# A hybrid attention and pooling layer on one core: the means of the pooling mixer by two operations a product from values kept in DRAM, each gate's job behind its group's values, and pooling sums later

## The chip, the cores and the metric

The kernel runs on one core of a Trainium2 chip. A core has a matrix engine (TensorE, here PE; its weight loads are PEld), a vector engine (VectorE, DVE), an engine for activations, copies and casts (ScalarE, ACT), a general engine (GpSimd, POOL) and one that in this kernel only starts transfers (SyncE, SP). Each engine works through its own instructions in a fixed order and waits, where it must, for the others by semaphores. Transfers (DMAs) are started by an instruction in the queue of SP, POOL or ACT. The metric is the time of the whole program in microseconds on the device; lower is better.

## The reference

One layer, 1024 tokens, width 2048, everything in float32:

```python
h = x @ w_in + b_in
q, k, v, g_attn, u_pool, g_pool = split(h)
a = banded_sink_attention(q, k, v, sinks, bias, valid) * silu(g_attn)
b = multiscale_pool(u_pool, w_pool, pool_scale) * silu(g_pool)
mix = concatenate([a, b]) @ w_out
ple = sigmoid(x @ w_gate_ple) * (p @ w_ple)
out = layer_norm(2 ** 0.25 * x + mix + ple, ln_gain, ln_bias)
```

The pooling mixer has 1024 channels in four groups of 256. Group g takes the mean over the last 2, 4, 8 or 16 tokens (fewer at the start), subtracts the token itself, multiplies by a 256 x 256 matrix of the group and by a scale for each channel.

## The kernel before

**Products.** Activations lie with channels on the 128 partitions and tokens along the free dimension. A float32 matrix is split into a rounded part and a rest (names ending in h and l), and a product of two such matrices is three matmuls (`mm3`, L182 to L184: high by high, high by low, low by high). The large matrix products go by a Strassen scheme with seven products in place of eight. A *job* (class `Job`) takes two blocks of 128 output channels and half of the 2048 input channels, for 1024 tokens in most stages; it is seven products (`product`), and each product is four input blocks by three matmuls of 128x512, so twelve matmuls. Two or three jobs may run interleaved in one group (`run_group`); otherwise a job is its own group. A product's result is taken from PSUM by `gather`: four of a job's seven by a copy on ACT (L402), three by an add on DVE (L125, `part<-part,qa` or `qb`). The weights arrive as `raw`; `make_unit` forms Strassen's sums of them on DVE, casts the high part on ACT (`wh`, L736) and subtracts on DVE (`wl`, L125), four units ahead of their use.

**Stages.** Stage 1 and 2 make the first parts of q, k, v over the two halves of the input channels, stage 2 also the second-half part of all other blocks, which is stored in DRAM (`h`, `g`) and added to the first-half part in stage 3 by an accumulating DMA of POOL (`finished`, L415). Attention itself runs beside stage 2, between about 180 and 700 us. Stage 3 (about 690 to 1125 us) is 20 jobs in the order of the list `rest`: pooling gate and pooling values of group 0 interleaved, then gate 3, values 3, gate 2, values 2, values 1, gate 1; then eight jobs of the embedding gate (`wgate`), then four of the attention gates, the last two interleaved. Stage 4 multiplies by w_out for the second input half, stages 5 and 6 for the first half in two cuts of the tokens (768 and 256), with the sums of squares and the output of the norm beside them.

**The clock of the plan.** The order is written by the program itself: each product is a tick (`tick`), `after(n, f)` emits f's instructions n products later, and `later(n, f)` does that with each of them held behind the last matmul, ACT copy and DVE add of the products so far. When a job ends, its `done` is called by `later(job.wait, ...)`, wait being 4 products for most jobs and 3 for the last pair of stage 3, so that the accumulating DMA can land. `load` starts a DMA from SP's queue, `aside` from POOL's. Engine order and buffers are then settled at build time; a tile drawn from a pool waits until a buffer of that pool is free.

**The steps that the change touches.**
- `set_from` makes the operand sets of stage 1 on DVE (`sub`) and ACT; step s2 splits t1 and forms t2.
- `ple_half` (L778) is early work of the embedding in stage 1; its result leaves PSUM by an ACT copy `b22h<-tr`, `b22h<-pv` (L736 is the helper `copy`).
- `set_kept` loads and splits the operand sets of stage 3's first group.
- `pool_u` (called as `done` of the value jobs): for each of two blocks and both halves of the tokens, ACT adds the bias (L128), DVE doubles the window by one, two, three or four adds (`s<-s`, L125), subtracts the token (L698), and the result is split (ACT `e<-s`, DVE `e<-s,e`). All of it is emitted in one tick. `mix(g)` follows ten or eleven products later: 24 matmuls into the two `sc` banks, each result multiplied with the gate that `gate_pool` stored (`sgp`).
- `pool_sums` fetches four pieces of the mixer's result (`s<-cc`) two ticks into the embedding's jobs 4, 6, 8, 10, forms four differences (`s<-s,s`) on DVE two ticks after that and stores them (`pt<-s`) for stage 4.
- `embed`, `embed_ahead`, `embed_w`: the embedding's gate, its fetched values, its weights.
- `gate_attn`: silu on ACT (L666), two multiplications on DVE by the fetched attention output (`gate_ahead`, `s<-pre`), and a store `cc<-part` from POOL's queue.
- `norm_square` (L921), `norm_scale`, `norm_out`: the norm's steps in stages 5 and 6.

Results of jobs lie in five buffers `part`; small tiles of stage 3 in 16 buffers `s` and six `e`, ten `s` at its end.

Of the kernel before, what the change touches and what calls it, by code (L numbers as in the profile page):

```python
# [25 lines left out]
F32R = mybir.dt.float32r  # L26
# [25 lines left out]
RAWS = 5  # L52
EARLY = (0, 1, 6, 7)


# [9 lines left out]
class Layer:  # L65
# [203 lines left out]
    def set_from(self, get, F, keep=None, first=None, by=None):  # L269
# [47 lines left out]
        def s2():  # L317
            split("t1")
            sub("t2", "b22", "t1", None if keep else "t1")

# [34 lines left out]

    def pool_sums(self, i, m, keep):

        at = [(4 + i, 0), (4 + i, 1), (6 + i, 0), (6 + i, 1)]
        r = []

        def make():
            b11, b12, b21, b22 = r
            self.tt(b11, b12, b11, ALU.subtract)
            self.tt(b12, b22, b12, ALU.subtract)
            self.tt(b22, b22, b11, ALU.subtract)
            self.tt(b21, b21, b22, ALU.subtract)
            for u, t in (("t1", b11), ("t3", b12), ("t2", b22), ("t4", b21)):
# [295 lines left out]

    def gate_attn(self, j, c):
        nc = self.nc
        nc.scalar.activation(c, c, AF.Silu, bias=self.c(C_BIN + GA0 + j))  # L666
# [9 lines left out]

    def pool_u(self, j, c):
        nc, g = self.nc, j // 2
        w = 2 << g
        out = []  # L680
        for h in range(2):
            u = self.slot()
            if h == 0:
                nc.gpsimd.memset(u[:, 0:16], 0.0)
            else:
                self.ident_act(u[:, 0:16], c[:, 0, T - 16 :], self.c(C_BIN + U0 + j))
            self.ident_act(u[:, 16:], c[:, h], self.c(C_BIN + U0 + j))
            cur, d, first = u, 1, 1
            while d < w:
                nxt = self.slot()  # L690
                end = 2 * d == w
                f = 16 if end else first
                self.tt(nxt[:, f:], cur[:, f:], cur[:, f - d : T + 16 - d], ALU.add)
                cur, d = nxt, 2 * d
                first = first + d
            if h == 0:
                self.tt(cur[:, 16 : 16 + 16], cur[:, 16 : 16 + 16], self.c(C_HEAD + 16 * g, 16), ALU.mult, nc.gpsimd)
            nc.vector.scalar_tensor_tensor(out=cur[:, 16:], in0=cur[:, 16:], scalar=1.0 / w, in1=u[:, 16:],  # L698
                                           op0=ALU.mult, op1=ALU.subtract)
            out.append(self.split(cur[:, 16:], 2 * (j % 2) + h < 3))  # L700
        self.diff[j] = out
        if j % 2:
            f = slice((g % 2) * T, (g % 2) * T + T)
            self.after(4, lambda: self.got.update({("wp", g): self.fetch(self.wpool[g // 2][:, f])}))
            self.later(8, lambda: self.got.update({("wp", g): self.split(self.got["wp", g])}))
            late = 3 if g == 1 else 0
            self.after(6 + late, lambda: self.got.update({("sg", g): [[self.fetch(self.sgp[2 * g + e][:, h * T : h * T + T]) for e in range(2)] for h in range(2)]}))
            self.later(10 + late // 2, lambda: self.mix(g))

# [68 lines left out]
    def ple_half(self, n, h, tags):  # L778
# [13 lines left out]
        for b in range(2):  # L792
            if h:
                self.aside(self.ple[2 * i + b], self.ple_out[(2 * n + b) % 4].rearrange("p h t -> p (h t)"))

    def embed_in(self, r=None):
# [191 lines left out]
    def run(self):  # L988
# [12 lines left out]
        self.sgp = [self.scratch("sgp") for _ in range(8)]  # L1001
        self.r = [self.scratch("r") for _ in range(NB)]
        self.ple = [self.scratch("ple") for _ in range(NB)]
        self.ple_raw, self.turn = {}, {}
# [31 lines left out]
        def consume(w):  # L1036
            def done(b, c):
                if w is wgate:
                    self.embed(b, c)
                elif b >= GP0:  # L1040
                    self.gate_pool(b - GP0, c)
                elif b >= U0:
                    self.pool_u(b - U0, c)
                else:
                    self.gate_attn(b - GA0, c)
            return done
# [20 lines left out]
        s6[-1].mean = True  # L1067
        for j in s4[-2:]:
            j.wait = 6
# [136 lines left out]
        for i in range(n3):  # L1206
# [7 lines left out]
            if i == n3 - 2:  # L1214
# [137 lines left out]
        self.second_done = lambda b, c: self.norm_square(two, b, c)  # L1352
        self.later(3, lambda: self.norm_scale(one, 2))
        for j in range(NB):
            self.later(6 + 18 * j // 16, lambda j=j: self.norm_out(one, j))
        for i in range(8):
# [60 lines left out]
```

## Time and profile before

| | |
|---|---|
| time, median of 3 runs | 1468.27 us |
| the three runs | 1466.94, 1468.27, 1468.92 us |
| profiled execution, own time | 1470.93 us |
| its span, first to last instruction | 1469.2 us |
| mean granted TensorE clock | 0.996 |
| DVE, ACT, POOL busy | 76%, 54%, 20% of the span |
| HBM read, written | 205.62 MB, 94.37 MB |

The page of the profile gives busy times of each engine. PE counts as busy while any matmul is in its pipeline, and two neighbouring matmuls overlap, so short losses don't show as idle time. They show in the number of matmuls that fall into a stretch. The waits of the trace say which instruction stood and whose end released it; a row reads "engine, tile and line <- releaser: us in total, times, longest".

### The profile page before, as it was taken

The page shows a single profiled execution, that of the slowest core. Times are in us where ns is not written, and L with a number is a line of the kernel's source. Part 1 is how long each engine was busy: PE and PEld are TensorE (multiplying, and loading weights), DVE is VectorE, ACT ScalarE, POOL GpSimd, SP SyncE. Part 2 cuts the span into 40 slices and gives each one's busy share as a digit, 9 for nine tenths or more (in the row PEclk, how much of TensorE's full clock was granted, in tenths as well). Part 3 has the DMA queues.
Part 4 walks back from the last instruction along what each step waited for, and adds up shares of the span by engine and source line. Part 5 has one row for each costly group of instructions (what it writes and reads, how often), then busy time and mean ns, then how long its engine had stood idle before and what let it go on. Part 6 is the DMA issues. An engine that isn't in the chain of part 4 may idle for free. (4 is left out here: it accounts for less than half of the span.)

```text
span 1469.2 us, 20535 instructions
## 1 busy us (share of the span) xinstructions
PE 1437.4 (98%) x6930; PEld 1214.9 (83%) x6930; DVE 1120.8 (76%) x2031; ACT 787.3 (54%) x1564; POOL 294.4 (20%) x416
## 2 busy tenths in 40 slices
PE   9999999999999999999999999999999999999996
PEld 7788888888888888887887788788877788899996
DVE  6869578878788797888668785867678566987786
ACT  6546376565575665566545444333456333554475
POOL 1000203332233333223010111211011111111223
PEclk9999999999999999999999999999999999999998
DMA  9463875554456554557765669899698678595475
GB/s 354 173 241 117 244 216 177 178 167 151 138 179 213 188 172 165 186 180 265 191 190 149 166 179 320 260 288 275 189 335 278 184 179 232 134 263 124 120 243 200
DMA packets 109993, 301.35 MB, mean 205 GB/s; under 512 B 12544, under 2 KB 18048, under 8 KB 109888
## 3 DMA queue, kind: packets, MB, share of 16 engines
q1 hardware_dynamic: 84672, 217.46, 43.4%
q0 software_dynamic: 21888, 75.25, 21.2%
q10 hardware_dynamic: 3328, 7.34, 1.5%
q8 instruction: 54, 0.88, 0.2%
q14 instruction: 51, 0.42, 0.1%
HBM read 205.62 MB, written 94.37 MB: 204 GB/s over the span
## 5 line engine op out<-in xcount | busy, mean ns | idle before, releaser
L736 ACT CAST wh<-raw 128x512 fp32r<-128x512 f32 x428 | 263.9, 619 | 400.5 <-PE qa L183 125.6
L125 DVE TENSOR_TENSOR wl<-raw,wh 128x512 fp32r<-128x512 f32 x428 | 300.0, 704 | 102.7 <-ACT wh L736 97.6
L402 ACT COPY part<-qa 128x512 f32<-128x512 f32 (+1 forms) x180 | 103.7, 576 | 74.9 <-PE qa L184 74.4
L620 POOL TENSOR_SCALAR_AFFINE_SELECT s<-s 128x512 fp32r<-128x512 f32 x128 | 102.4, 812 | 132.0 <-ACT s L613 96.5
L125 DVE TENSOR_TENSOR part<-part,qb 128x512 f32<-128x512 f32 (+1 forms) x120 | 81.1, 676 | 44.7 <-PE qb L184 40.1
L182 PE MATMUL qa<-b11h,wh 128*128 128x512 f32 (+2 forms) x292 | 109.4, 375 | 0.4 <-ACT wh L736 0.4
L182 PE MATMUL qb<-b21h,wh 128*128 128x512 f32 (+2 forms) x292 | 109.3, 374 | 0.0
L184 PE MATMUL qa<-b11h,wl 128*128 128x512 f32 (+2 forms) x292 | 108.8, 373 | 0.0
L184 PE MATMUL qb<-b21h,wl 128*128 128x512 f32 (+2 forms) x292 | 108.8, 372 | 0.0
L183 PE MATMUL qa<-b11l,wh 128*128 128x512 f32 (+2 forms) x292 | 108.7, 372 | 0.0
L183 PE MATMUL qb<-b21l,wh 128*128 128x512 f32 (+2 forms) x292 | 108.6, 372 | 0.0
L182 PE MATMUL qb<-t1h,wh 128*128 128x512 f32 (+1 forms) x260 | 100.8, 388 | 3.4 <-DVE part L125 1.6
L182 PE MATMUL qa<-t2h,wh 128*128 128x512 f32 (+1 forms) x260 | 101.1, 389 | 3.0 <-ACT wh L736 1.8
L182 PE MATMUL qa<-t4h,wh 128*128 128x512 f32 (+1 forms) x260 | 100.7, 387 | 2.7 <-DVE part L125 2.7
L182 PE MATMUL qa<-t3h,wh 128*128 128x512 f32 (+1 forms) x260 | 100.6, 387 | 1.6 <-ACT part L402 1.6
L184 PE MATMUL qa<-t2h,wl 128*128 128x512 f32 (+1 forms) x260 | 100.1, 385 | 1.8 <-DVE wl L125 1.8
L182 PE MATMUL qb<-b22h,wh 128*128 128x512 f32 (+1 forms) x260 | 100.5, 386 | 0.5 <-ACT part L402 0.5
L183 PE MATMUL qa<-t3l,wh 128*128 128x512 f32 (+1 forms) x260 | 99.8, 384 | 0.0
L184 PE MATMUL qb<-t1h,wl 128*128 128x512 f32 (+1 forms) x260 | 99.7, 384 | 0.0
L184 PE MATMUL qa<-t4h,wl 128*128 128x512 f32 (+1 forms) x260 | 99.7, 384 | 0.0
L183 PE MATMUL qa<-t2l,wh 128*128 128x512 f32 (+1 forms) x260 | 99.7, 383 | 0.0
L184 PE MATMUL qb<-b22h,wl 128*128 128x512 f32 (+1 forms) x260 | 99.7, 383 | 0.0
(327 smaller groups left out, 3567.2 us busy)
## 6 DMA issues: line engine op xcount, KB each, us to landing
raw<-in_win SPq DMA_DIRECT2D x65, 512.0 KB, 4.3
h<-part SPq DMA_DIRECT2D x34, 512.0 KB, 2.9
part<-h POOLq DMA_DIRECT2D x34, 512.0 KB, 6.6
cw<-in_wout SPq DMA_DIRECT2D x64, 256.0 KB, 3.0
raw<-in_wgate SPq DMA_DIRECT2D x32, 512.0 KB, 4.4
raw<-wc SPq DMA_DIRECT2D x32, 512.0 KB, 4.3
s<-in_x SPq DMA_DIRECT2D x44, 256.0 KB, 5.9
wc<-cw SPq DMA_DIRECT2D x32, 256.0 KB, 2.4
```

What stands on the lines that cost most here:

```text
L125: return (eng or self.nc.vector).tensor_tensor(out=out, in0=a, in1=b, op=op)
L182: mm(ps, wh, xh, start=start, stop=False, skip_group_check=True)
L183: mm(ps, wh, xl, start=False, stop=False, skip_group_check=True)
L184: return mm(ps, wl, xh, start=False, stop=stop, skip_group_check=True)
L402: self.mark("ACT", self.nc.scalar.copy(out=dst, in_=ps))
L620: nc.gpsimd.affine_select(out=o4, in_=a4, pattern=[[0, 4], [sign, P]], compare_op=ALU.is_ge, fill=0.0, base=0 if side else -1, channel_mul ...
L736: ins = self.nc.scalar.copy(out=out, in_=a)
```

## The change

In stage 1, t2 is formed two products later; and the ACT copies after one of the early embedding pieces are held in order behind its output. The operand sets of stage 3's first group are split half a set at a time, in two neighbouring products. The differences of `pool_sums` are formed two each at 7 and 8 ticks in place of four at 4. `pool_u` stores the values with their bias in DRAM (`ud`) from SP, keeps the first block on chip, fetches the second one back, and emits the chain of adds, subtraction and rest two operations a product; the mix follows when they are through, or 13 or 14 products after. In the order of stage 3's jobs the values of groups 3 and 2 come ahead of their gates. The two jobs of attention gates ahead of the last pair wait five products, fetch the attention output earlier, and store from SP one product later. The embedding's weights are split four products after their fetch, not two. The jobs of stage 5 but the last two wait six products for their sum, and the norm's first scale is spread one product later.

```diff
+POOL_MIX = {3: 13, 2: 14, 1: 13}
...
         def s2():
             split("t1")
-            sub("t2", "b22", "t1", None if keep else "t1")
+            if first:
+                self.later(2, lambda: sub("t2", "b22", "t1", None))
+            else:
+                sub("t2", "b22", "t1", None if keep else "t1")
...
         def step(i):
             u = UNITS[BESIDE[i]]
-            self.split_unit(u, r.pop(u))
-            fetch(i + 2)
+            pieces = r.pop(u)
+            self.split_unit(u, [])
+            for n in range(2):
+                self.split_part(u, n, pieces[n])
+
+            def rest():
+                for n in range(2, 4):
+                    self.split_part(u, n, pieces[n])
+                fetch(i + 2)
+
+            if i:
+                self.after(1, rest)
+            else:
+                rest()
...
-        self.later(4, make)
+        for second in range(2):
+            self.later(7 + second, lambda second=second: make(second))
...
-    def gate_attn(self, j, c):
+    def gate_attn(self, j, c, soon):
...
-        self.aside(self.cc[j // 2][:, j % 2], c.rearrange("p h t -> p (h t)"))
+        store = lambda by: by(self.cc[j // 2][:, j % 2], c.rearrange("p h t -> p (h t)"))
+        if soon:
+            self.after(1, lambda: store(self.load))
+        else:
+            store(self.aside)
...
     def pool_u(self, j, c):
+        g = j // 2
+        self.ident_act(c, c, self.c(C_BIN + U0 + j))
+        if j % 2 == 0:
+            self.pool_first = [self.slot() for _ in range(2)]
+            self.nc.gpsimd.memset(self.pool_first[0][:, 0:16], 0.0)
+            self.nc.scalar.copy(out=self.pool_first[1][:, 0:16], in_=c[:, 0, T - 16 :])
+            for h in range(2):
+                self.nc.scalar.copy(out=self.pool_first[h][:, 16:], in_=c[:, h])
+        self.load(self.ud[j], c.rearrange("p h t -> p (h t)"))
+        if j % 2 == 0:
+            return
+        self.diff[j - 1], self.diff[j] = [None, None], [None, None]
+        begin = max(0, self.pool_free - self.clock)
+        n = 0
+        for k in range(4):
+            todo = self.window(j - 1 + k // 2, k % 2, k)
+            if k == 2:
+                n = max(n, 2 * (6 - begin))
+            if k > 1:
+                self.after(max(1, begin + n // 2 - 4), todo.pop(0))
+            for op in todo:
+                self.later(begin + n // 2 + 1, op)
+                n += 1
+        end = begin + (n + 1) // 2 + 1
+        self.pool_free = self.clock + end
+        f = slice((g % 2) * T, (g % 2) * T + T)
+        at = max(end, POOL_MIX.get(g, 0))
+        self.after(at - 6, lambda: ...
+        self.later(at - 1, lambda: ...
+        self.after(at - 4, lambda: ...
+        self.later(at + 1, lambda: self.mix(g))
+
+    def window(self, j, h, k):
...
+        def fetch():
+            u = s["u"] = self.slot()
+            if h:
+                self.load(u, self.ud[j][:, T - 16 : 2 * T])
...
+        def double(d, begun):
+            cur = s.get("cur", s["u"])
+            nxt = s["cur"] = self.slot()
+            f = 16 if 2 * d == w else begun
+            self.tt(nxt[:, f:], cur[:, f:], cur[:, f - d : T + 16 - d], ALU.add)
...
+        def less():
...
+            nc.vector.scalar_tensor_tensor(out=cur[:, 16:], in0=cur[:, 16:], scalar=1.0 / w, in1=s["u"][:, 16:],
                                            op0=ALU.mult, op1=ALU.subtract)
...
+            nc.scalar.copy(out=s["hi"], in_=cur[:, 16:])
+
+        def low():
+            self.lo(s["lo"], s["cur"][:, 16:], s["hi"])
...
-            self.later(2, lambda: make(r))
+            self.later(4, lambda: make(r))
...
-        rest = [gp[0], u[0], gp[3], u[3], gp[2], u[2], u[1], gp[1]] + [(wgate, *p) for p in pairs(0, 8)] + ga
+        rest = [gp[0], u[0], u[3], gp[3], u[2], gp[2], u[1], gp[1]] + [(wgate, *p) for p in pairs(0, 8)] + ga
...
-            j.wait = 3 if j in s3[-2:] else 4
-            j.ahead = self.embed_ahead if j.w is wgate else (lambda b: self.gate_ahead(b - GA0)) if j is s3[-3] else None
+            j.wait = 3 if j in s3[-2:] else 5 if j in s3[-4:-2] else 4
+            j.ahead = self.embed_ahead if j.w is wgate else None
...
-        for j in s4[-2:]:
+        for j in s4[-2:] + s5[:-2]:
             j.wait = 6
...
+            if at == (2, 1):
+                self.turn.pop("ACT")
             if at in turn:
-                self.ple_half(*turn[at], (("tr", 1), ("pv", 1)))
+                out = self.ple_half(*turn[at], (("tr", 1), ("pv", 1)))
+                if at == (2, 0):
+                    self.turn["ACT"] = out
...
-                for b in s3[-4].b:
-                    self.after(1, lambda b=b: self.gate_ahead(b - GA0))
+                for n, b in enumerate(s3[-4].b + s3[-3].b):
+                    self.after((1, 1, 5, 6)[n], lambda b=b: self.gate_ahead(b - GA0))
...
-        self.later(3, lambda: self.norm_scale(one, 2))
+        self.later(3, lambda: self.norm_scale(one, 3))
```

More of the change, by code (lines that the diff above doesn't have):

```diff
@@ new lines, in pool_u @@
+        end = begin + (n + 1) // 2 + 1
+        self.pool_free = self.clock + end
+        f = slice((g % 2) * T, (g % 2) * T + T)
+        at = max(end, POOL_MIX.get(g, 0))
+        self.after(at - 6, lambda: self.got.update({("wp", g): self.fetch(self.wpool[g // 2][:, f])}))
+        self.later(at - 1, lambda: self.got.update({("wp", g): self.split(self.got["wp", g])}))
+        self.after(at - 4, lambda: self.got.update({("sg", g): [[self.fetch(self.sgp[2 * g + e][:, h * T : h * T + T]) for e in range(2)] for h in range(2)]}))
@@ L701, in pool_u @@
[L701 to L708, printed above, removed]
+        s = {"u": None}
@@ new lines, in window @@
+        ops = []
+        def fetch():
+            u = s["u"] = self.slot()
+            if h:
+                self.load(u, self.ud[j][:, T - 16 : 2 * T])
+            else:
+                nc.gpsimd.memset(u[:, 0:16], 0.0)
+                self.load(u[:, 16:], self.ud[j][:, 0:T])
+        def double(d, begun):
[3 more added lines that the diff above has]
+            self.tt(nxt[:, f:], cur[:, f:], cur[:, f - d : T + 16 - d], ALU.add)
+            if 2 * d == w and h == 0:
+                self.tt(nxt[:, 16 : 16 + 16], nxt[:, 16 : 16 + 16], self.c(C_HEAD + 16 * g, 16), ALU.mult, nc.gpsimd)
@@ new lines, in less @@
+        def less():
+            cur = s["cur"]
+            extra = k < 3
+            nc.vector.scalar_tensor_tensor(out=cur[:, 16:], in0=cur[:, 16:], scalar=1.0 / w, in1=s["u"][:, 16:],
+                                           op0=ALU.mult, op1=ALU.subtract)
+            s["hi"], s["lo"] = ((self.extra if extra else self.slot)(F32R)[:, :T] for _ in range(2))
+            nc.scalar.copy(out=s["hi"], in_=cur[:, 16:])
+        def low():
+            self.lo(s["lo"], s["cur"][:, 16:], s["hi"])
+            self.diff[j][h] = (s["hi"], s["lo"])
@@ L710, in mix @@
+        if k > 1:
+            ops.append(fetch)
+        else:
+            s["u"] = self.pool_first[k]
+        d, begun = 1, 1
+        while d < w:
+            ops.append(lambda d=d, begun=begun: double(d, begun))
+            d *= 2
+            begun += d
+        return ops + [less, low]
     def mix(self, g):
```

40 lines of the change are left out of this document (13 added, 27 removed).

## The prediction

> **What bounds the kernel now.** I read the page first, then the counts of matmuls by stretch, then the waits of PE.
>
> ```profile
> PE 1437.4 (98%) x6930; PEld 1214.9 (83%) x6930; DVE 1120.8 (76%) x2031; ACT 787.3 (54%) x1564; POOL 294.4 (20%) x416
> ```
>
> PE is the bound. What a change of order can win is the time in which PE stands, and "98% busy" hides part of it. Stretches of 80 us show it (columns: PE busy and number of matmuls, then PEld, DVE, ACT, POOL likewise, granted clock, DMA share, GB/s):
>
> ```profile
> 80.00:160.00 80.00, 80.00 (x355) 66.24 (x354) 62.15 (x82) 39.67 (x60) 1.80 (x2) 1.00 0.50 169
> 720.00:800.00 80.00, 79.57 (x350) 65.19 (x349) 57.38 (x92) 42.38 (x71) 11.44 (x20) 1.00 0.65 163
> 800.00:880.00 80.00, 77.83 (x337) 62.47 (x336) 64.80 (x102) 35.73 (x64) 12.89 (x24) 1.00 0.68 189
> 880.00:960.00 80.00, 75.97 (x330) 61.38 (x329) 54.54 (x87) 30.29 (x49) 12.91 (x19) 1.00 0.91 282
> 960.00:1040.00 80.00, 80.00 (x352) 65.70 (x351) 50.49 (x81) 29.86 (x48) 9.80 (x14) 1.00 0.93 285
> 1080.00:1160.00 80.00, 76.23 (x331) 61.43 (x331) 60.48 (x85) 43.70 (x63) 10.27 (x15) 1.00 0.82 267
> 1160.00:1240.00 80.00, 80.00 (x355) 66.24 (x354) 48.42 (x68) 27.35 (x47) 14.03 (x20) 1.00 0.78 210
> 1420.00:1440.00 20.00, 19.93 (x165) 19.32 (x164) 20.00 (x34) 18.78 (x29) 11.25 (x21) 1.00 0.98 337
> ```
>
> Undisturbed, 355 matmuls pass in 80 us: 0.225 us each, 2.70 us a product of twelve. Against 355 the pooling stretch (720 to 880) misses 5 + 18 = 23, or 5.2 us; 880 to 960 misses 25, 5.6 us, though PE is idle only 4.0 us (each stop also costs some tenths of a microsecond after the restart); 1080 to 1160 misses 24, 5.4 us. The clock is 1.00 throughout, so these are waits. PE's waits from 690 to 1160 us:
>
> ```profile
> PE qa L182 <- DVE part L125: 2.5, 3, 1.7
> PE sc L182 <- DVE part L125: 1.7, 1, 1.7
> PE qa L182 <- ACT wh L736: 1.5, 1, 1.5
> PE qa L182 <- ACT part L402: 1.4, 2, 1.2
> PE qb L182 <- DVE part L125: 1.2, 1, 1.2
> PE qa L184 <- DVE wl L125: 1.1, 2, 0.7
> PE qb L182 <- ACT wh L736: 0.9, 1, 0.9
> PE qb L182 <- ACT part L402: 0.5, 1, 0.5
> PE sc L182 <- ACT s L153: 0.4, 2, 0.2
> ```
>
> Each names an ordinary step of a product (a gather, a weight's cast or rest), never a DMA: PE waits for ACT or DVE, which were held by something else in their own queues. Outside this stretch, the places that the change touches are these (the first two before 60 us, then two at 1370 to 1400, one after 1400):
>
> ```profile
> PE tr L182 <- ACT b22h L736: 1.4, 1, 1.4
> ...
> PE qb L182 <- DVE part L125: 0.4, 1, 0.4
> ...
> PE qb L182 <- DVE d L125: 0.8, 1, 0.8
> PE qa L182 <- ACT wh L736: 0.3, 1, 0.3
> ...
> PE sc L937 <- ACT q L954: 0.3, 1, 0.3
> ```
>
> **The change part by part.**
>
> *Stage 1.* Idle 1.4 + 0.4, with two restarts 2.2 us. The ACT copy that frees the bank `tr` stands behind a cast of t2, which needs t2 from DVE. Holding the casts behind that copy, and t2 two products back, undoes both waits; but the work of DVE stays, and DVE is the busy engine there. Between nothing gained, or 1 us lost where t2 becomes the late one, and 2.2 gained I take **1.2**.
>
> *First set of stage 3.* The 0.9 wait for `wh` stands behind four casts of t2; with two of them in the next product it goes. With the restart 1.1 at most; 0.9 taken.
>
> *Pooling.* The groups of 720 to 880 us (count, then busy us and mean ns, then idle before) show for DVE
>
> ```profile
> L698 DVE SCALAR_TENSOR_TENSOR s<-s,s 128x512 f32<-128x512 f32 x16 | 11.0, 688 | 1.2 <-POOL s L125 0.4 <-POOL s L684 0.4
> ...
> L125 DVE TENSOR_TENSOR e<-s,e 128x512 fp32r<-128x512 f32 x12 | 8.2, 684 | 0.4 <-ACT e L153 0.4
> ```
>
> and on ACT
>
> ```profile
> L128 ACT ACTIVATE s<-part,cst 128x512 f32<-128x512 f32 x16 | 11.5, 716 | 0.0
> L673 ACT ACTIVATE part<-part,cst 128x1024 f32<-128x1024 f32 x8 | 8.8, 1145 | 0.0
> L153 ACT CAST e<-s 128x512 fp32r<-128x512 f32 x12 | 7.5, 622 | 8.2 <-DVE s L698 5.2 <-PE sc L183 3.0
> ```
>
> By the code there are 16 subtractions, 40 adds and 16 rests: 72 operations of about 0.69 us, 50 us of DVE, before and after alike. Group 3's 24 are emitted in one tick: 16.5 us, six products of DVE. A gather's add has about one product to finish before its bank is used again, so it and the weights' rests come late. Two a product remove the burst. Do they fit? In 1160 to 1240 DVE does the products' own work alone, 68 operations in 355 / 12 = 29.6 products, so 2.3 a product; with two more 4.3. Where DVE is full (1420 to 1440) 34 operations pass in 20 us, 4.6 in a product. So it fits with 7% to spare. ACT: 16 x 0.72 and 8 short ones before; after, eight of 1024 columns, 1.15 each by the silu's row, and eight plain copies: the same within 2 us, off the path with ACT at half load. SP gains eight stores of 512 KB and eight fetches of 256 KB, 6.3 MB in 160 us, 39 GB/s on 163 to 189, where the DMA share of 0.65 to 0.68 rises to about 0.8; cover is the 4 products (10.8 us) between fetch and first use. If that cover is gone DVE stands in its queue, and gathers with it. Bounds: all 5.2 gained; or, if every product that holds a subtraction and its rest also waits a cast of 0.62 us with nothing else to do, 16 x 0.62 = 9.9 lost. Nearest is the row `e<-s,e`: its twelve rests idled 0.4 us in all. I take **3.2**. The mixes come at almost the same ticks (28, 41, 53, 66 in place of 27, 41, 55, 63 of the stage), and the gates are still there ahead of them (gate 3 done at 31, fetched at 36), so the new order of jobs costs nothing by itself.
>
> *Pooling sums.* Two products (5.4 us) lie between the fetch and the differences. DVE's wait for it, 910 to 950 us:
>
> ```profile
> DVE s L125 <- DMA s<-cc: 11.3, 3, 5.9
> ```
>
> PE's later stop in the timeline, and the landing of the pieces (880 to 960 us, median us):
>
> ```profile
> 946.27 0.51 PE L182 MATMUL sc<-e,s 128*128 128x512 f32 x1 [1.68 <-DVE part L125]
> ```
> ```profile
> s<-cc SPq DMA_DIRECT2D x12, 256.0 KB, 10.2
> ```
>
> A piece takes 10.2 us (DMA share 0.91), so DVE stands 11.3 us, and the embedding's own gathers stand behind it: 1.7 us at 946, as much at 922 (the longest of the first PE row). Differences 5 and 6 products after the fetch (13.5 and 16.2 us) find their data. Of the 5.6 us of this stretch, the waits for ACT `part` of 0.5 and 0.2, with restarts 1.3, have other causes (a sigmoid behind the accumulating DMA, the casts of p): 4.3 can go, 3.8 taken. The four buffers are held four products longer; of 16 some eleven are drawn in a job, so a fetch may wait, which is bounded by the 0.7 us that 960 to 1040 still misses.
>
> [...]
>
> *Attention gates.* 5.4 us. The waits behind them, on ACT from 1080 to 1112 us, and landings between 1085 and 1110:
>
> ```profile
> ACT part L402 <- DMA cc<-part: 2.5, 1, 2.5
> ACT part L666 <- DMA part<-h: 2.1, 1, 2.1
> ```
> ```profile
> s<-pre SPq DMA_DIRECT2D x7, 256.0 KB, 9.1
> cc<-part POOLq DMA_DIRECT2D x2, 512.0 KB, 8.2
> ```
>
> Wait 5 takes the silu off the accumulating DMA's landing (2.1 us against 2.7 more); the earlier fetch helps the multiplications. The last pair (wait 3, unchanged) keeps its `qb <- DVE part` of 1.2, 1.5 with the restart: 3.9 can go. The store now goes one product later and through SP. A gather's copy waits for its buffer `part` until that store has landed (the 2.5). Queued behind the store on SP are the last pair's eight fetches, 2.1 MB, 8 us at the 267 GB/s of 1080 to 1160, which before went ahead; that shortens its landing. Ends: 3.9 gained, or 2.7 + (9.1 - 8.2) = 3.6 us more waiting, making -2.0. Taken 2.6.
>
> *Stage 5 and the norm.* 0.8 + 0.3 idle, 1.5 with restarts: squares on ACT behind an accumulating DMA; two more products cover it, 1.1 taken (0 to 1.5). The 0.3 of the spread (0.7 with its slow restart): 0.4 (0 to 0.7).
>
> **Sum**: 1.2 + 0.9 + 3.2 + 3.8 + 2.6 + 1.1 + 0.4 = 13.2. Every moved step falls into products that had no extra work. The nine rows above hold 14 waits of 0.8 us on average; I charge three new ones, 2.4. Net 10.8: from the profiled execution's 1470.93 to 1460.1. The median of the runs lies 2.7 below that execution, so **1457.5 us**.
>
> **The rivals.**
>
> *The next wait takes the place.* PE's waits are short because ACT and DVE lie just behind; half the gain goes to whichever is next: 1468.3 - 5.4 = 1462.9. For it: DVE busy 65 of 80 us at 800 to 880. Against: 960 to 1040 with 0.93 of DMA and the same kinds of work loses only 3 matmuls.
>
> *SP's store of the gates lands late.* The end given above: 2.6 becomes -2.0, 1462.1. For it: SP's landings of 9.1; against: the eight fetches behind it.
>
> [...]
>
> *DVE overfull in the pooling* (ends slower). Each operation of a chain needs the one before it, and `later` holds each pair behind the product's gather. If DVE cannot fill the gap left by one cast, the load is 4.3 + 1 against 4.6 a product, 0.7 x 0.6 = 0.4 us too much, and over 36 products 15 us are lost where 3.2 were gained: 1475.7. It decides from 0.3 us a product (10.5 us lost). For it: only 7% to spare; against: DVE's order is settled at build time with other work between, as the idle of 0.4 shows. A milder form, 0.2 a product, ends at about the time before.
>
> *Nothing happens.* The edits shift emission, the engine order is settled afterwards; if it comes out as before, 1468.3.
>
> **How the numbers follow.** Forecast (1452 to 1461.5) 0.50; next wait 0.14; late store 0.12; overfull 0.13; mild form or no effect 0.11. A median of this kernel can be told from no change by about 0.2%, 2.9 us. Faster by more: 0.76; within: 0.11; slower: 0.13. If everything that can go goes, 18.9 us, 1449.4 would result; I leave that and the slow side out: 1452 to 1468.
>
> **What would show it.** Right: 720 to 880 and 880 to 960 reach about 350 matmuls per 80 us; no `DVE s <- DMA s<-cc` above 1 us; `ACT part <- DMA cc<-part` gone or below 2.5; no `b22h` wait before 60. Wrong: waits for `part` or `wl` spread over the whole of 740 to 870, a DVE wait for the fetched values, SP waiting for ACT ahead of raw weights, or a longer `cc` wait at 1105.

## The result, and the profile after

| | before | after |
|---|---|---|
| time, median of 4 runs each (before's three and one more) | 1468.6 us | 1461.32 us |
| lowest and highest | 1466.94, 1470.84 | 1460.25, 1462.15 |
| profiled execution, its span | 1470.93, 1469.2 | 1460.25, 1458.5 |

The ratio after / before is 0.9946, with an interval of [0.9933, 0.9960]: faster by 7.3 us between the medians. The two profiled executions lie 10.7 us apart, because before's was at the top of its spread and after's the lowest of its four. In after's code most lines have moved: L126 is before's L125 (the DVE helper), L183 to L185 the three matmuls, L421 the gather's copy, L685 the gates' silu, L805 the cast helper, L434 the accumulating DMA.

The page's busy times say almost nothing of the change, PE is at 98% as before:

```profile
PE 1435.3 (98%) x6930; PEld 1216.8 (83%) x6930; DVE 1120.4 (77%) x2031; ACT 788.9 (54%) x1560; POOL 292.6 (20%) x412
```

The counts of matmuls by stretch do. The windows of after (columns as in the prediction):

```profile
720.00:800.00 80.00, 80.00 (x352) 65.71 (x352) 57.55 (x92) 45.09 (x74) 10.80 (x20) 1.00 0.83 231
800.00:880.00 80.00, 79.89 (x351) 65.61 (x351) 62.67 (x100) 34.91 (x58) 13.55 (x23) 1.00 0.74 208
880.00:960.00 80.00, 79.92 (x350) 65.41 (x349) 60.09 (x96) 33.42 (x53) 11.99 (x18) 1.00 1.01 324
...
1080.00:1160.00 80.00, 76.27 (x328) 62.26 (x327) 56.15 (x78) 43.03 (x63) 10.54 (x15) 0.98 0.81 243
```

From 720 to 960 us 350 or more matmuls now pass in each 80 us, where 337 and 330 did in the worst two. But 1080 to 1160, where the gates were to gain, has 328, even fewer than before's 331, and its granted clock is 0.98. PE's waits from 690 to 1160 us shrink from nine rows to three:

```profile
PE qb L183 <- ACT wh L805: 2.0, 1, 2.0
PE qa L183 <- ACT part L421: 1.8, 1, 1.8
PE qb L183 <- DVE part L126: 0.7, 1, 0.7
```

The two large ones are both in the attention gates' stretch: 1.8 at 1096 us is at the matmul where before waits 1.2 for ACT `part`, 2.0 at 1125 is new.

A sharper measure than idle time is worked out from the trace's matmul starts: for every matmul the distance to the next start, less the usual distance of its shape (226.5 ns for 512 columns, 174 for 384, 118, 109 and 110 for 256, 128 and 1). The sum over a stage is what PE loses there, in waits, restarts and lower clock. Stages are cut at the same matmul in every kernel, and named by the time at which that stood in before:

```
us of PE lost        0-60  680-720 720-880 880-960 1080-1160 1360-1400 1400-end
before               5.02    1.38    5.00    5.55    5.38      1.99     5.55
after                3.67    1.20    1.21    0.82    6.00      1.90     5.29
e1_sums_at_4         4.25    1.15    0.61    8.27    8.86      1.62     5.31
e2_pool_in_one       3.13    0.83    4.57    0.28    8.65      1.85     5.32
e3_gates_before      3.68    0.87    0.78    0.89    5.06      1.78     5.26
e4_store_pool        4.43    0.78    0.61    0.73    4.85      1.57     5.31
e5_sums_alone        4.79    1.96    4.64    0.88    5.96      1.81     5.63
e6_sixth_part        4.03    0.78    0.59    0.69    6.76      1.66     5.54
e7_stage1_before     3.73    0.78    0.54    1.28    6.23      1.76     5.54
e8_s5_wait4          3.60    1.72    0.63    0.69    5.03      1.78     5.33
e9_six_wait4         4.59    0.81    0.58    0.91    1.74      1.82     5.18
e10_six_wait5        3.73    0.77    0.57    0.69    0.25      1.68     5.51
e11_six_gates_before 4.31    0.73    0.57    0.66    2.89      2.12     5.28
e12_six_wait5_sp     4.41    0.79    0.58    0.69    0.86      2.10     5.62
```

Over the whole program before loses 42.6 us and after 32.3; these 10.3 are nearly all of the 10.7 between the two profiled executions. Pooling (5.00 to 1.21) and pooling sums (5.55 to 0.82) make 8.5 of them. One caution: 400 to 680 us, which no edit touches, lost between 6.7 and 9.7 us over these profiles, so a difference of a few tenths, or of one whole profile, is no evidence. In 1080 to 1160 us, which the edits of e1, e2, e7 and e8 don't touch, after and these four lost 6.00, 8.86, 8.65, 6.23 and 5.03 us.

### The profile page after: what moved, and what is told of

Read it like the earlier page. It is cut to its first block, busy times and chain, and to the rows that moved or that the text cites. A ratio compares the mean times of both kernels' runs of the same rounds, so it can differ in the third digit from the quotient of the medians.

```text
span 1458.5 us, 20547 instructions
## 1 busy us (share of the span) xinstructions
PE 1435.3 (98%) x6930; PEld 1216.8 (83%) x6930; DVE 1120.4 (77%) x2031; ACT 788.9 (54%) x1560; POOL 292.6 (20%) x412
## 4 chain that ended last, share of the span: by engine, by line
PE 64%; issue 22%; DVE 5%; POOL 4%; ACT 3%; DMA 2%; POOLq 0%; SPq 0%; ACTq 0%; DVEq 0%
PE qa L183 11%; PE qa L185 11%; PE qa L184 11%; PE qb L183 8%; PE qb L184 8%; PE qb L185 8%; POOL part L434 2%; PE sc L594 1%; PE pv L652 1%; DVE s L126 1%; DVE wl L126 1%; PE tr L630 1%; DMA part<-h 1%; DVE part L126 1%; PE sc L183 1%
## 5 line engine op out<-in xcount | busy, mean ns | idle before, releaser
L805 ACT CAST wh<-raw 128x512 fp32r<-128x512 f32 x428 | 264.0, 619 | 395.8 <-PE qa L184 143.5
L126 DVE TENSOR_TENSOR wl<-raw,wh 128x512 fp32r<-128x512 f32 x428 | 300.1, 705 | 108.6 <-ACT wh L805 105.5
L421 ACT COPY part<-qa 128x512 f32<-128x512 f32 (+1 forms) x180 | 103.9, 577 | 78.6 <-PE qa L185 76.2
L126 DVE TENSOR_TENSOR part<-part,qb 128x512 f32<-128x512 f32 (+1 forms) x120 | 81.1, 676 | 46.4 <-PE qb L185 39.3
L183 PE MATMUL qa<-b11h,wh 128*128 128x512 f32 (+2 forms) x292 | 109.4, 375 | 0.8 <-ACT wh L805 0.8
L183 PE MATMUL qb<-b21h,wh 128*128 128x512 f32 (+2 forms) x292 | 109.2, 374 | 0.0
L185 PE MATMUL qa<-b11h,wl 128*128 128x512 f32 (+2 forms) x292 | 108.8, 373 | 0.0
L185 PE MATMUL qb<-b21h,wl 128*128 128x512 f32 (+2 forms) x292 | 108.6, 372 | 0.0
L183 PE MATMUL qb<-t1h,wh 128*128 128x512 f32 (+1 forms) x260 | 101.3, 390 | 3.5 <-ACT wh L805 2.0
L183 PE MATMUL qa<-t3h,wh 128*128 128x512 f32 (+1 forms) x260 | 100.6, 387 | 2.0 <-ACT part L421 2.0
L183 PE MATMUL qa<-t2h,wh 128*128 128x512 f32 (+1 forms) x260 | 100.8, 388 | 1.1 <-ACT part L421 0.5
L185 PE MATMUL qa<-t2h,wl 128*128 128x512 f32 (+1 forms) x260 | 99.9, 384 | 0.7 <-DVE wl L126 0.7
L183 PE MATMUL qb<-b22h,wh 128*128 128x512 f32 (+1 forms) x260 | 100.4, 386 | 0.0
L184 PE MATMUL qb<-t1l,wh 128*128 128x512 f32 (+1 forms) x260 | 100.3, 386 | 0.0
L185 PE MATMUL qb<-t1h,wl 128*128 128x512 f32 (+1 forms) x260 | 100.2, 386 | 0.0
L183 PE MATMUL qa<-t4h,wh 128*128 128x512 f32 (+1 forms) x260 | 100.1, 385 | 0.0
L185 PE MATMUL qb<-b22h,wl 128*128 128x512 f32 (+1 forms) x260 | 99.7, 383 | 0.0
L184 PE MATMUL qb<-b22l,wh 128*128 128x512 f32 (+1 forms) x260 | 99.7, 383 | 0.0
```

The costliest lines, as they stand in the source:

```text
L126: return (eng or self.nc.vector).tensor_tensor(out=out, in0=a, in1=b, op=op)
L183: mm(ps, wh, xh, start=start, stop=False, skip_group_check=True)
L184: mm(ps, wh, xl, start=False, stop=False, skip_group_check=True)
L185: return mm(ps, wl, xh, start=False, stop=stop, skip_group_check=True)
L421: self.mark("ACT", self.nc.scalar.copy(out=dst, in_=ps))
L805: ins = self.nc.scalar.copy(out=out, in_=a)
```

## The experiments

The ratios below are to the kernel before, of several runs each; "loses" refers to the table above.

**e1_sums_at_4**: the changed kernel with the sums of before.

```diff
-        for second in range(2):
-            self.later(7 + second, lambda second=second: make(second))
+        self.later(4, make)
```

> The changed kernel with the four differences of the pooling sums formed together 4 products into the job, as before; all else stays. Theory (they waited for a fetch of some 10 us and PE's gathers behind them): DVE waits 5 us or more for s<-cc, the stretch 870 to 950 us loses 15 to 20 matmuls again, and the time rises by about 4 us, 1461.3 to 1465. Rival (the later split of the embedding's weights, or the fewer collisions of the new pooling order, gave that gain): the stretch stays within 5 matmuls of full and the time within 1 us of 1461.3.

1469.0 us, 0.9997 [0.9985, 1.001]: 7.7 us slower than after, the whole win gone. Its twelve runs reach from 1464.85 us at a mean granted clock of 0.996 to 1473.07 at 0.992, and the profiled one is this slowest. DVE's wait, PE's wait from 900 to 930 us, and two windows of this kernel:

```profile
DVE s L126 <- DMA s<-cc: 7.9, 2, 6.0
```
```profile
PE qa L183 <- DVE part L126: 4.6, 1, 4.6
```
```profile
880.00:960.00 80.00, 75.36 (x319) 60.94 (x318) 54.71 (x87) 30.71 (x50) 12.00 (x18) 0.96 0.96 296
920.00:925.00 5.00, 3.96 (x9) 3.15 (x10) 5.00 (x9) 0.00 (x0) 0.59 (x1) 0.50 0.84 285
```

The mechanism is the predicted one: DVE stands for the fetched pieces, the gather's add stands behind it, PE stands for the gather. But a stop of 4.6 us is followed by a granted clock of 0.50: the stretch loses 8.27 us against 0.82. This profile has half clock in two more places, both between 1080 and 1160 us (8.86 lost), so its figures are more than a usual run of e1 loses.

**e5_sums_alone**: the same edit the other way round, on the kernel before, and nothing else.

```diff
-        self.later(4, make)
+        for second in range(2):
+            self.later(7 + second, lambda second=second: make(second))
```

> The kernel of before with one part of the change alone: the differences of the pooling sums at 7 and 8 ticks. Theory (parts add up; DVE's wait for s<-cc cost 4 us there): PE's loss from 880 to 960 us falls from 5.5 to about 1.5 us, time 4 us under the kernel of before, ratio 0.997. Rival (most of the gain came only with the new pooling order, as the 7.7 us lost in e1_sums_at_4 suggest): less than 2 us, ratio above 0.9985.

1465.74 us, 0.9975 [0.9963, 0.9987]: 3.7 us under before by this ratio. The stretch has the matmuls that after has there, and loses 0.88:

```profile
880.00:960.00 80.00, 79.73 (x351) 65.48 (x350) 55.49 (x89) 33.08 (x54) 12.84 (x19) 1.00 0.97 302
```

So the sums need nothing of the rest of the change.

**e2_pool_in_one**: the changed kernel with `pool_u` and the order of jobs of before.

```diff
-        rest = [gp[0], u[0], u[3], gp[3], u[2], gp[2], u[1], gp[1]] + ...
+        rest = [gp[0], u[0], gp[3], u[3], gp[2], u[2], u[1], gp[1]] + ...
```

> The changed kernel with pool_u and the order of stage 3's jobs as before: all operations of a group in one product, nothing stored in DRAM. Theory (the burst of up to 24 DVE operations held gathers and weights): 720 to 880 us misses about 20 matmuls again against 7 now, and the time rises by 3 to 4 us to about 1465. Rival (the gain there is paid back by 6.3 MB more traffic and later fetches elsewhere): the stretch loses as much, but the rest gets faster, and the time stays within 1 us of 1461.3.

1464.37 us, 0.9969 [0.9956, 0.9982], 3.05 us over after (the intervals just overlap). The windows are nearly before's again:

```profile
720.00:800.00 80.00, 79.56 (x350) 65.20 (x349) 57.51 (x91) 43.37 (x72) 10.76 (x19) 1.00 0.64 167
800.00:880.00 80.00, 78.03 (x340) 62.83 (x339) 63.99 (x101) 34.31 (x61) 14.38 (x26) 1.00 0.65 184
```

340 against 351 matmuls, with DVE as busy in both (64.0 and 62.7 us): the burst costs, not the sum of DVE's work. This run undoes the spacing, the way through DRAM and the order of the jobs together; which of them is needed was not tried.

**e3_gates_before**: the changed kernel with the attention gates' wait, fetches and store of before.

```diff
-            j.wait = 3 if j in s3[-2:] else 5 if j in s3[-4:-2] else 4
+            j.wait = 3 if j in s3[-2:] else 4
...
-                    self.gate_attn(b - GA0, c, b in s3[-4].b + s3[-3].b)
+                    self.gate_attn(b - GA0, c, False)
```

> The changed kernel with the attention gates as before: store from POOL's queue at once, wait of 4 products, the third last job's attention output fetched when that job ends. Theory (this part of the change only moved the stop: the two stops before 1100 us shrank, the one behind the last pair grew from 1.5 to 3.8 us): 1080 to 1160 us loses about 5.2 us in place of 5.9, time 1460.5, within 1 us of 1461.3. Rival (the part gained its 2.6 us as predicted, and something else lost them): time rises to about 1464.

1460.55 us, 0.9939 [0.9921, 0.9957]: the same as after. This part of the change brought nothing that can be told from the scatter (5.06 us lost against 6.00).

**e4_store_pool**: only the store goes back to POOL's queue at once; wait 5 and early fetches stay.

```diff
-                    self.gate_attn(b - GA0, c, b in s3[-4].b + s3[-3].b)
+                    self.gate_attn(b - GA0, c, False)
```

> The changed kernel, but the two jobs of attention gates ahead of the last pair store from POOL's queue at once; the longer wait and the earlier fetch stay. Theory (the store in SP's queue holds SP until the multiplications are done, so ten later fetches run just when the last pair's accumulating DMAs do, and the last silu waits 4.1 us): the silu's wait falls below 2 us, the stop of 2 us near 1125 us to below 1.5, time about 1459. Rival (the fetches' new places and the wait of 5 do it alone): no change, 1461.3.

1460.29 us, 0.9935 [0.9916, 0.9954], not to be told from after. The stop at 1125 went, but the other stood for 2.6 us, and 3.4 us at half clock came behind it. In the five profiles with after's code in this stretch (after, e1, e2, e7, e8) there is a stop each time at the matmul of 1125, of 1.8 to 2.7 us; the one at the matmul of 1096 scatters from 1.0 to 2.5. PE's only wait in 1080 to 1160, and ACT's from 1080 to 1128:

```profile
PE qa L183 <- ACT part L421: 2.6, 1, 2.6
```
```profile
ACT part L421 <- DMA cc<-part: 3.4, 2, 2.8
ACT part L685 <- DMA part<-h: 3.0, 2, 2.5
```

In after a silu of the last pair stood longer for its accumulating DMA. Behind it stood DVE's multiplications by its result, in DVE's queue behind these the sum for PE's next weight, and that weight's cast. The same ACT waits, then the timelines of ACT, DVE and PE and two windows of after:

```profile
ACT part L685 <- DMA part<-h: 6.9, 2, 4.1
...
ACT part L421 <- DMA cc<-part: 2.3, 1, 2.3
```
```profile
1121.56 1.15 ACT L685 ACTIVATE part<-part,cst 128x1024 f32<-128x1024 f32 x1 [4.14 <-DMA part<-h]
1124.73 0.62 ACT L805 CAST wh<-s 128x512 fp32r<-128x512 f32 x1 [2.02 <-DVE s L126]
```
```profile
1122.75 1.29 DVE L126 TENSOR_TENSOR part<-s,part 128x512 f32<-128x512 f32 x2 [3.56 <-ACT part L685]
1123.96 0.68 DVE L126 TENSOR_TENSOR s<-raw 128x512 f32<-128x512 f32 x1
```
```profile
1123.05 0.39 PE L185 MATMUL qb<-b21h,wl 128*128 128x512 f32 x1
1125.39 0.69 PE L183 MATMUL qb<-t1h,wh 128*128 128x512 f32 x1 [1.95 <-ACT wh L805]
1125.87 0.63 PE L184 MATMUL qb<-t1l,wh 128*128 128x512 f32 x1
1126.30 0.63 PE L185 MATMUL qb<-t1h,wl 128*128 128x512 f32 x1
```
```profile
1125.00:1130.00 5.00, 4.61 (x13) 3.70 (x14) 5.00 (x10) 4.17 (x7) 0.26 (x1) 0.66 0.27 107
1130.00:1135.00 5.00, 5.00 (x23) 4.03 (x22) 3.76 (x7) 1.71 (x4) 1.28 (x3) 1.00 0.53 210
```

Read it downwards: 4.1 us of ACT for the DMA, 3.6 us of DVE for the silu, then two multiplications and the sum `s<-raw`. The cast `wh<-s` waits 2.0 us for that sum on an ACT that is free again, and starts 0.66 us before PE goes on. PE stands 1.95 us, and then its matmuls are 0.43 us apart in place of 0.23 until the clock is back. How does the store's queue reach the last pair's DMA? The last pair's four accumulating DMAs took longer to land with the store in SP's queue. Their landing in after (1106 to 1116 us) and in e4 (1110 to 1119):

```profile
part<-h POOLq DMA_DIRECT2D x4, 512.0 KB, 9.4
```
```profile
part<-h POOLq DMA_DIRECT2D x4, 512.0 KB, 5.8
```

The medians of these four are 9.3 to 9.9 us in the six profiles with the store in SP's queue (after, e1, e2, e7, e8, e12) and 5.8 to 8.3 in the eight with it in POOL's. SP's timeline in after, and in e4, shows the last fetches of the attention output:

```profile
1103.41 0.90 SPq L140 DMA_DIRECT2D s<-pre  x2
1104.35 0.90 SPq L140 DMA_DIRECT2D two<-pt  x2
1105.30 1.12 SPq L140 DMA_DIRECT2D s<-pre  x2
```
```profile
1089.14 0.99 SPq L140 DMA_DIRECT2D s<-pre  x2
```

With the store in SP's own line these fetches are issued 16 us later (1106 against 1090), just ahead of the accumulating DMAs, the first of which starts at 1106.45. That the DMAs land later is measured; that these fetches are what delays them is argued from the order.

**e6_sixth_part**: e4 with a sixth buffer `part` from the third-last job of stage 3 on, paid for by two slots.

```diff
-                self.slots = self.work_pool("slots1", 10, work)
+                self.slots = self.work_pool("slots1", 8, work)
+                six[:] = 5 * [pp] + [self.work_pool("p7", 1, work)]
```

> As e4_store_pool (gates' store from POOL's queue), and a sixth buffer part from the third last job of stage 3 on, for two fewer small tiles there (8 of 10). Theory (the copy of a product of the last pair waits for the store of the third last job, because a part buffer is missing; PE stands 2.6 us, and then runs 3.4 us at half clock): both go, 1080 to 1160 us loses about 1 us in place of 4.9, time 1456 to 1457. Rival (DVE and ACT are full there and the next wait follows at once): the stretch loses 3 us or more, time 1459 to 1460.

1460.44 us, 0.9933 [0.9920, 0.9947]: no gain. The buffer's wait is gone, and the silu's took over. PE's only wait in 1080 to 1160, then ACT's first row to 1128:

```profile
PE qb L183 <- ACT wh L805: 3.5, 1, 3.5
```
```profile
ACT part L685 <- DMA part<-h: 6.2, 4, 2.5
```

The rival was right here: the next wait took the gain, whole.

**e9_six_wait4, e10_six_wait5**: e6 with the last pair's wait at 4, or 5, products; removes the stop that e6 uncovered.

```diff
-            j.wait = 3 if j in s3[-2:] else 5 if j in s3[-4:-2] else 4
+            j.wait = 5 if j in s3[-2:] else 5 if j in s3[-4:-2] else 4
```

> As e6_sixth_part, and the last pair of stage 3 waits 4 products for its accumulating DMAs, not 3. Theory (there the silu waits for a DMA that lands too late, and the casts of weights stand behind it on ACT; PE stands 3.5 us and runs 6.8 us at half clock): one product, 2.7 us, more covers most of it; 1080 to 1160 us loses 1 to 2.5 us in place of 6.8, time 1455 to 1457. Rival (the DMAs are simply late against PE, and the work behind them, DVE's multiplications and the operand set of stage 4, becomes late instead): 4 us or more lost, 1459 to 1460.

> As e9_six_wait4 with 5 products for the last pair. Theory: as e9 or 0.5 us better, the silus never wait. Rival (the longer the wait, the later the last mixer results and the tail of stage 3 on DVE, which meet the first products of stage 4): worse than e9 by 1 us or more.

1456.79 us, 0.9921 [0.9908, 0.9934], and 1456.40 us, 0.9915 [0.9902, 0.9928]. The stretch loses 1.74, and 0.25. PE's only wait from 690 to 1160 in e10, and its window:

```profile
PE qb L183 <- DVE part L126: 0.3, 1, 0.3
```
```profile
1080.00:1160.00 80.00, 80.00 (x354) 65.95 (x353) 60.52 (x84) 44.39 (x65) 12.75 (x19) 1.00 0.86 260
```

354 matmuls, against 355 in the undisturbed stretch at 80 us. The five us that the stretch loses in before went with both cures; the pair's longer wait without the sixth buffer wasn't tried.

**e11_six_gates_before**: e10, with the earlier two jobs' wait and fetches as before.

```diff
-            j.wait = 5 if j in s3[-2:] else 5 if j in s3[-4:-2] else 4
+            j.wait = 5 if j in s3[-2:] else 4
```

> As e10_six_wait5, with the wait of 4 and the fetches of the two jobs ahead as before the change. Theory (these two of the change's parts matter, once the buffer and the pair's wait are out of the way: the stops near 1070 and 1088 us, 2 us together in e3_gates_before, come back): 1.5 to 2 us slower than e10. Rival (they are worth nothing): equal within 0.7 us.

1457.89 us, 0.9930 [0.9918, 0.9942]: 1.5 us over e10, with overlapping intervals; the trace says more, 2.89 us lost against 0.25. So wait 5 and the early fetches are worth something once the way behind them is free, and nothing while it isn't (e3).

**e12_six_wait5_sp**: e10 with the store in SP's queue.

```diff
-                    self.gate_attn(b - GA0, c, False)
+                    self.gate_attn(b - GA0, c, b in s3[-4].b + s3[-3].b)
```

> As e10_six_wait5, but with the two jobs' gates stored from SP one product later, as the change has it. Theory (with the buffer there and the last pair waiting 5, nothing waits for that store any more; it only orders SP's later fetches): within 1 us of e10's 1456.4, the stretch 1080 to 1160 us below 1.5 us lost. Rival (SP held by the store makes the operand set of stage 4 or the last fetches late): 2 us or more slower, new waits after 1100 us.

1456.15 us, 0.9909 [0.9893, 0.9926], equal to e10. With buffer and wait there, the queue of the store doesn't matter. It has the lowest median of all, 5.2 us under after, and its interval lies clear of after's; 6.00 - 0.86 = 5.1 us in this stretch explain it.

**e7_stage1_before**: the changed kernel with stage 1 as before.

```diff
-            if first:
-                self.later(2, lambda: sub("t2", "b22", "t1", None))
-            else:
-                sub("t2", "b22", "t1", None if keep else "t1")
+            sub("t2", "b22", "t1", None if keep else "t1")
...
-                out = self.ple_half(*turn[at], (("tr", 1), ("pv", 1)))
-                if at == (2, 0):
-                    self.turn["ACT"] = out
+                self.ple_half(*turn[at], (("tr", 1), ("pv", 1)))
```

> The changed kernel with stage 1 as before: t2 formed at once, no order of the ACT copies after the early embedding piece. Theory (the two stops of before near 36 and 40 us are due to these): they come back, 2.2 us of PE time between 20 and 60 us in place of 0, and the time rises by 1 to 2 us, since the first 20 us vary by a microsecond. Rival (the work only moves): the stretch 0 to 60 us loses the same in sum, 3.7 us, time 1461.3.

1461.57 us, 0.9950 [0.9934, 0.9965], equal to after, and my theory fell. The windows of before, after and e7:

```profile
0.00:20.00 20.00, 18.59 (x79) 14.99 (x80) 10.89 (x16) 13.78 (x23) 2.85 (x12) 1.00 0.89 322
20.00:60.00 40.00, 38.19 (x167) 30.98 (x166) 35.02 (x44) 26.04 (x41) 3.38 (x6) 1.00 0.74 295
```
```profile
0.00:20.00 20.00, 18.04 (x74) 14.62 (x75) 10.98 (x17) 14.31 (x24) 3.27 (x12) 1.00 0.89 335
20.00:60.00 40.00, 40.00 (x178) 33.12 (x177) 35.90 (x45) 26.27 (x40) 2.60 (x5) 1.00 0.72 289
```
```profile
0.00:20.00 20.00, 17.90 (x74) 14.27 (x75) 11.11 (x17) 14.39 (x24) 3.25 (x12) 1.00 0.91 335
20.00:60.00 40.00, 40.00 (x177) 32.93 (x177) 35.90 (x45) 26.09 (x40) 2.38 (x5) 1.00 0.73 288
```

With before's code in stage 1, e7 still has after's picture: more lost ahead of 20 us, nothing between 20 and 60. By the timelines the first subtraction of the set on `two`, which in most profiles ends a short wait for x, starts at 27.6 us in before, 26.0 in e7 and 26.1 in after. The other profiles confirm that the larger stop, the wait for `b22h`, goes with that start and not with the edit. It is there in the six profiles in which the subtraction starts at 27.4 us or later: at 40 us in before and e5, and at 45 us, with 0.6 to 1.2 us, in e4, e9, e11 and e12, which have the edit. It is missing in the eight in which it starts by 27.1 us. What makes the start early or late varies from run to run.

**e8_s5_wait4**: stage 5's wait back at 4.

```diff
-        for j in s4[-2:] + s5[:-2]:
+        for j in s4[-2:]:
```

> The changed kernel with the jobs of stage 5 waiting 4 products as before, not 6. Theory (the wait of 6 removed the ACT waits for the accumulating DMA, but the stop of 1 us at the last pair of stage 5 has another cause, DVE's own queue): PE's loss from 1360 to 1400 us stays at 1.9 us, time within 1 us of 1461.3. Rival (the waits moved a stop away that would be larger by now): the loss rises by 1 us or more.

1461.41 us, 0.9944 [0.9931, 0.9957], equal to after. PE's waits from 1360 to 1400 us, in after and then in e8:

```profile
PE qb L183 <- DVE d L126: 0.8, 1, 0.8
PE qa L183 <- ACT wh L805: 0.4, 1, 0.4
```
```profile
PE qb L183 <- DVE d L126: 0.8, 1, 0.8
PE qa L183 <- ACT wh L805: 0.3, 1, 0.3
```

Both are nearly before's rows (0.8 and 0.3). The longer wait did shorten what ACT's squares `q` stand for that DMA from 1360 to 1400 us, from 3.9 us in before and 3.8 in e8 to 1.0 in after, but the stop of 0.8 stayed: the squares and their DMA have no part in it. In the 4 us ahead of it DVE works without a gap of 0.2 us in after and e8, so the stop belongs to DVE's own queue.

## Why the prediction was right or wrong

The forecast of 1457.5 us was 3.8 us too fast, inside its range; direction and the two large terms held, one term failed, and two small ones had the wrong cause. The number by itself proves little: 1461.3 is at the upper end of the bounds that the forecast had for itself (1452 to 1461.5), and nearer to the 1462.9 of the first rival than to 1457.5.

- **Pooling, 3.2 forecast: right.** 3.8 in its stretch, 3.05 by e2. "Two a product remove the burst" is what the windows show; the overfull DVE of the rival did not come, and there is no sign of it: PE has no wait for `part` or `wl` from 740 to 870 us. DVE's load was the same, its order wasn't.
- **Pooling sums, 3.8 forecast: right in mechanism.** No `DVE s <- DMA s<-cc` is left, though a piece takes not much less than the 10.2 us of before; the landings in after from 880 to 960 us:

```profile
s<-cc SPq DMA_DIRECT2D x12, 256.0 KB, 8.6
```

  Five and six products, 13.5 and 16.2 us, cover that. By e5 it is worth 3.7. The stretch gained 4.7, also some of the 1.3 that I had given to other causes. What undoing it costs, 7.7 by e1, I put too low by half (a rise of about 4 was expected), since I counted waits at full clock: e1's profile has a granted clock of 0.96 from 880 to 960 us and lost 8.27 us there, where before, at 1.00, lost 5.55.
- **Attention gates, 2.6 forecast: failed, -0.6 measured** between the two profiles, which is inside the scatter: the stretch loses 5.06 to 5.96 us without this part (before, e3, e5) and 5.03 to 8.86 with it (after, e1, e2, e7, e8). The first step that failed is "Wait 5 takes the silu off the accumulating DMA's landing". The 2.1 us counted there are the wait of the second silu of the third last job, and after has it still, no shorter (of the 6.9 us in two waits above, 2.7 are this one and 4.1 the last pair's). ACT's timeline in before, then in after:

```profile
1095.93 1.15 ACT L666 ACTIVATE part<-part,cst 128x1024 f32<-128x1024 f32 x1 [2.13 <-DMA part<-h]
```
```profile
1084.98 1.16 ACT L685 ACTIVATE part<-part,cst 128x1024 f32<-128x1024 f32 x1 [2.71 <-DMA part<-h]
```

  Wait 5 moved only the fourth last job's silus, which had not waited: they start 63 matmuls behind their first accumulating DMA, in place of 51. The third last job's start 42 behind theirs, where before had 43; why the longer wait did not move them stays open. The second step is the sentence "The last pair (wait 3, unchanged) keeps its `qb <- DVE part` of 1.2". In after this wait is gone, but a silu of the pair became the one that waits longest for its accumulating DMA (4.1 us), and PE stood 1.95 us and ran at half clock after it. The buffer's wait also stayed (2.3 against 2.5 of ACT). I had priced the rival "SP's store lands late" for this place; it is not that. The landing from 1085 to 1110 us in after:

```profile
cc<-part SPq DMA_DIRECT2D x2, 512.0 KB, 7.3
```

  POOL's took 8.2 in before, and e12 equals e10. What SP's store does cost is the later landing of the accumulating DMAs (9.4 us in after, 5.8 in e4). So this is the rival "the next wait takes the place", here alone.
- **Stage 1, 1.2 forecast: no effect of the edits** (e7). I read two stops of one execution as a property of the order; the larger one comes and goes with the start of one early subtraction. The sign "no `b22h` wait before 60" was met in after by luck: four later profiles with the edit have that wait.
- **Stage 5, 1.1 forecast: 0.1.** The wait row named DVE's `d`, and I put it down to ACT and a DMA behind it, with no row that joins the two.
- **First set and norm, 0.9 and 0.4 forecast: 0.2 and 0.3.** In the first set one wait for `wh` of 0.9 gave way to one for `part` of 0.7. After the norm's edit the 0.3 wait for `q` is gone; a further 0.4 for `wh` stands there instead. Neither edit was undone by itself, and gains of this size are inside the scatter.
- **The charge of 2.4 for new waits** was of the right kind. Pooling, sums, first set and norm measured 3.8 + 4.7 + 0.2 + 0.3 = 9.0; the gates' -0.6, and 0.4 more lost between 1160 and 1360 us (1.72 to 2.13), leave 8.0, near the 7.3 between the medians, though the smaller of these figures are single profiles'. The rest of the profiled pair's 10.3, 1.35 up to 60 us and 1.0 from 400 to 680, is scatter. So the charge covered 1 us of new waits, and its other 1.4 only part of the 4.9 of the three terms that brought nothing.

## What to carry to other kernels

Here the stops of a saturated engine came from the order of its neighbours' queues, so spread bursts evenly and count how long a fetch takes in the trace of its own stage (here 8.6 to 10.2 us for 256 KB) before its first use. Before a wait is priced as a gain, look for the next instruction in the same queue that waits for a similar transfer, and cure both: here the first jobs' wait and fetches brought nothing, nor did a buffer more, and with the last pair's wait they brought about 5 us. Ask also whether the edit moves the very instruction that waits. Undo each part by itself on the changed kernel; small stops that "disappeared" in one profile may only vary from run to run.

## What the hardware showed

Some stops of PE cost clock as well. The stops of 1.95 us (after), 2.64 (e4), 3.52 (e6) and 4.64 (e1) were each followed by a granted clock of 0.50, for 3.41 us after the first two and 6.83 after the others. Stops of 1.68 (before, at 946 us) and 1.78 (after, at 1096) had no such phase behind them. The window of after from 1125 to 1130, at 0.66 with 13 matmuls where 23 follow in the next, shows what it means: the eight matmuls that start in the phase lost 1.43 us, on top of the stop of 1.95.

The profiles of before and after also show when the clock changed. In after that was 1119.57, 1122.99 and 1443.84 us behind the first record of the clock, in before 1454.08: 328, 329, 423 and 426 times 3.4133 us. Cut into pieces of that length, the two profiles have, up to 1430 us, eight pieces in which PE stood for over 1 us. Half clock followed one of them, after's with 1.95 us. The other seven, five of before with 1.21 to 1.68 us and two of after with 1.07 and 1.18, were followed by full clock; after's stop of 1.78 us is among these, with 0.60 in one piece and 1.18 in the next. At the end of the programs, where other shapes run, half clock also followed pieces with 1.71 us (before) and 1.51 (after), so the standing time does not explain all of it.
